# Attention half of an encoder layer: the stores of weight sums, residual rows and kept split weights issued by GpSimd and not by SyncE

## The chip, the cores and the metric

The kernel runs on one core of one Trainium2 chip. The metric is device time in microseconds for one launch. Engines are named as the profile names them: PE is TensorE (PEld its weight loads), DVE is VectorE, ACT is ScalarE, POOL is GpSimd, SP is SyncE, which here does nothing but issue transfers (SPq is its queue).

## The reference, cut to what matters

The reference computes one layer of a streaming encoder, for a prompt of 2048 tokens and a sample of 64 tokens, with d_model 1024, all in fp32:

```
mod = silu(c) @ w_ada + b_ada                      # six columns of scales and shifts
h    = rmsnorm(x, g1) * (1 + sc1) + sh1
proj = h @ w_in                                    # u, q, k, v, o, gates
pool = causal window means (2, 4, 8, 16) of u, minus u, @ w_pool, * s_pool
hs   = mLSTM(q, k, v, gates), chunk by chunk, normalized per head, * sigmoid(o)
x    = x + gt1 * (concat(pool, hs) @ w_out)        # end of the attention half
h2   = rmsnorm(x, g2) * (1 + sc2) + sh2
up   = h2 @ w_up                                   # 2 x 2816 columns
conv = causal depthwise convolution of width 3 over up
x    = x + gt2 * ((silu(g) * a) @ w_down)          # the gated MLP
y    = rmsnorm(x, g_final)
```

The states of the pooling, of the mLSTM and of the convolution are outputs too. The attention half is everything up to the first new x.

## The kernel before

**Number format.** Every large product runs as three products of rounded parts: a matrix is split into a high part (ACT copies it rounded, L366) and a low part (DVE subtracts, L369), and PE forms high times high, high times low, low times high.

**Attention half.** The tokens are worked on in four groups of 512 (the last with the 64 sample tokens). For each group: the value projection (L1114), for each of four heads the projections of q, k and o (L423) with the mLSTM of the head before woven between them, four blocks for the pooling mixer, then the output projection, row by row (`outproj`). The mLSTM of a head ends with a normalizer: DVE makes a sum per token (L1309 to L1311), POOL raises it to the power -1/2 (L1313), DVE scales the head's rows with it (L1315), and PE transposes them (L1326). PE, DVE and POOL each work through their instructions in order.

**Weights.** A stream of units of 512 columns is read in a fixed order. `issue` starts the load on SP: an unsplit unit into one of four `raw` tiles (L350), a unit that was split before straight into one of six `wt` tiles (L355). `work_out` splits it, `get_unit` hands it to the product. In group 0 the projection weights come unsplit and, once used, their split halves are stored to DRAM by `keep` (L374, tensor `hl_kept`, 40 stores of some 512 KB), and groups 1 to 3 load them from there. `keep` also serves the MLP's weights (`wsplit`), at a time when `spare` is no longer empty.

**Weight sums.** For the MLP's products the kernel needs sums and differences of blocks of w_up. `up_sums` makes them in the background of groups 1 to 3: it loads four blocks into one of five `w4` tiles (L846), DVE adds and subtracts (L867 to L871), and `store` writes the tile to the tensor `wsum` (L856, 44 stores of 512 KB). Its instructions are pinned to program order among each other.

**Residual rows.** `outproj` loads a row of x into one of five `scr` tiles (L546), DVE adds the projection (L596) and the row is stored to `x2d` (L598, 32 stores).

**What sets the order.** In group 0's first part and in the MLP the order is as written. In the rest of the attention half a scheduler orders each engine's instructions by its own estimate of times, so that a store that moves to another engine can move others too. Transfers are issued in each engine's order: an instruction that waits holds everything behind it.

Of the kernel before, what the change touches and what calls it, by code (L numbers as in the profile page):

```python
# [9 lines left out]
F32 = mybir.dt.float32  # L10
# [49 lines left out]
def tile_layer(ctx: ExitStack, tc: tile.TileContext, xT, vecs, cst, rst, rowv, w_mod, w_ada, w_qkou, w_v, w_pool,  # L60
               w_out, w_up, w_down, st_C, st_pool, yT, o_pool, o_C, o_m, o_conv):
    nc = tc.nc
    act, dve, pool, pe = nc.scalar, nc.vector, nc.gpsimd, nc.tensor
# [16 lines left out]
    def mm_ps():  # L80
        return bank("mm")
# [12 lines left out]
    def scr():  # L94
        return sp.tile([P, TMAX], F32, tag="scr", name="scr")
# [142 lines left out]
    for g in range(NG):  # L238
        o = Grp()
# [48 lines left out]
    wsum = dr.tile([NF, P, 4, 512], F32, tag="wsum", name="wsum")  # L288
# [21 lines left out]
    for g in range(NFG):  # L310
        for (f0, f1_) in PARTS:
# [8 lines left out]
            for i, (n, k) in enumerate(order):  # L320
                if i == f1_ - f0 - 2:
                    stream += late
                c = f0 + k // 4 * 4
# [9 lines left out]
    class Unit:  # L333

        state = 0
        w = raw = None
# [34 lines left out]

    def keep(u):
        if u.keep is not None:
            nc.sync.dma_start(out=u.keep, in_=u.w.bitcast(F32)[:, :, :u.n])  # L374

    def pump():

# [10 lines left out]
    def get_unit():  # L388
        if not pend:
            issue()  # L390
        u = pend.pop(0)
        work_out(u)
        keep(u)
        return u.w
# [18 lines left out]
    def gemm(ps, W, mv, o, ks=None, order=None, late=None, ups=(1, 3, 4, 6)):  # L413
        order = order or list(range(len(mv)))
        ks = ks or order
        for k in ks:
            if late is not None and k == late:
                drain(0, 2)
            at = order.index(k)
            U = W.at(at // 4)  # L420
            for pi, (a, b) in enumerate(PASSES):
                for bi, (lo, hi) in enumerate(o.blks):
                    pe.matmul(ps[bi][:, :hi - lo], U[:, a, k % 4 * P:(k % 4 + 1) * P], mv[k][:, b, lo:hi],  # L423
                              start=(at == 0 and pi == 0), stop=(k == order[-1] and pi == 2))
            if at in (1, 2, 4, 6, 7):
                tick(0)
            if at in ups and not quiet:
                tick(4)
            if at in (1, 3, 5) and o.last and not spare:
                tick(1)  # L430
            if at in ((2, 5) if o.g else (4,)) and not quiet and not spare:
                tick(3)
            if spare and at in (1, 3, 4, 6):
                tick(1)
        for i in (1, 3):
            tick(i)
        for gen in list(bg[2]):
            if next(gen, 0) == 0:
                bg[2].remove(gen)
# [12 lines left out]
    def sq_acc(ssum, src, T, first):  # L452
        if first:
            act.activation(ssum[:, :T], src, AF.Square)
        else:
            s = scr()
            act.activation(s[:, :T], src, AF.Square)
            dve.tensor_tensor(out=ssum[:, :T], in0=ssum[:, :T], in1=s[:, :T], op=ALU.add)

    def ssum_tile():  # L460
        return sp.tile([P, TMAX], F32, tag="ssum", name="ssum", bufs=1)
# [11 lines left out]
    def col_sums(pt, src, o, first, last):  # L473
        for ti, (lo, n, s) in enumerate(o.chunks):
            c, d = ti % 4 * 32, ti // 4 * P
            pe.matmul(pt[c:c + 32, d:d + n], ones[:, 0:32], src[:, lo:lo + n], start=first and ti < 4, stop=last,
                      skip_group_check=True)
# [58 lines left out]
    x2d = dr.tile([KD, P, NTOK], F32, tag="x2d", name="x2d")  # L536
# [7 lines left out]
    def load_x(k, o):  # L544
        x = scr()
        nc.sync.dma_start(out=x[:, :o.T], in_=xT[k, :, o.t0:o.t0 + o.T])  # L546
        return x
# [14 lines left out]
    def stat2(o, ssum, squares, pt):  # L562
        for _ in range(5):
            yield
        out = RS2[:, 4 * o.g:4 * o.g + len(o.chunks)]
        for n, t in squares:
            col_sums(pt, t, o, n == 0, n == KD - 1)
            yield
        yield from rstd_rows(ssum, o, out, pt)
        yield  # L570

    def outproj(o, mix, between):

        order = [4, 5, 6, 7, 3, 2, 1, 0]
        ssum = None if o.last else ssum_tile()
        squares, pt = [], None
        nx = [load_x(n, o) for n in (0, 1)]
        for rows in [(0, 1)] + [(n,) for n in range(2, KD)]:
            xs = nx
            Ws = [Row() for _ in rows]  # L580
            pss = [[mm_ps() for _ in o.blks] for _ in rows]
            if len(rows) == 1:
                gemm(pss[0], Ws[0], mix, o, order=order, ups=(4,))
            else:
                for W, ps in zip(Ws, pss):
                    gemm(ps, W, mix, o, ks=order[:6], order=order)
                quiet.clear()
                for W, ps in zip(Ws, pss):
                    gemm(ps, W, mix, o, ks=order[6:], order=order, late=1)
            while squares and squares[0][0] < rows[0] - (rows[0] < KD - 1):  # L590
                n, t = squares.pop(0)
                col_sums(pt, t, o, n == 0, False)
            nx = [load_x(rows[-1] + 1, o)] if rows[-1] + 1 < KD else []
            for n, x, ps in zip(rows, xs, pss):
                for (bi, pa, pb, a, b, s) in o.pieces:
                    dve.scalar_tensor_tensor(out=x[:, a:b], in0=ps[bi][:, pa:pb], scalar=gt1(n, s), in1=x[:, a:b],  # L596
                                             op0=ALU.mult, op1=ALU.add)
                nc.sync.dma_start(out=x2d[n, :, o.t0:o.t0 + o.T], in_=x[:, :o.T])  # L598
            if rows[0] == 0:
                between()  # L600
                if o.last:
                    pt = small.tile([P, 512], F32, tag="bank", name="m2")
            for n, x in zip(rows, xs):
                if o.last:
                    t = scr() if n < KD - 1 else fscr("ssum")
                    act.activation(t[:, :o.T], x[:, :o.T], AF.Square)
                    squares.append((n, t))
                else:
                    sq_acc(ssum, x[:, :o.T], o.T, n == 0)
        bg[0].append(stat2(o, ssum, squares, pt))  # L610

    fgroups = []
    for g in range(NFG):
        o = Grp()
# [8 lines left out]
    def fscr(dt=F32):  # L623
        if dt in ("rb", "rbn", "ssum"):
            return spare[0].tile([P, FT], F32, tag=dt, name=dt)
        return spare[0].tile([P, FT], dt, tag="fscr", name="fscr", bufs=6)
# [5 lines left out]
    spare = []  # L632
# [201 lines left out]
    if True:  # L834
# [6 lines left out]
        def up_sums():  # L841

            def load(f, c):
                w = a1.tile([P, 4, 256], F32, tag="w4", name="w4", bufs=5)
                for i in range(2):
                    tc.keep_in_program_order(nc.sync.dma_start(out=w[:, 2 * i:2 * i + 2, :], in_=w_up[NF * i + f].rearrange(  # L846
                        "p (h c) -> p h c", h=2)[:, :, c:c + 256]))
                return w
            todo = [(f, c) for f in range(NF) for c in (0, 256)]
            pin = tc.keep_in_program_order  # L850
            nx = [load(*todo[0]), load(*todo[1])]
            done = []

            def store():
                f, c, w = done.pop(0)
                pin(nc.sync.dma_start(out=wsum[f, :, :, c:c + 256], in_=w))  # L856
            yield
            yield
            for i, (f, c) in enumerate(todo):
                w = nx.pop(0)  # L860
                yield
                yield
                if len(done) > 1:
                    store()

                a0, a1_, g0, g1 = (w[:, i, :] for i in range(4))
                pin(dve.tensor_tensor(out=g1, in0=g0, in1=g1, op=ALU.add))  # L867
                pin(dve.tensor_tensor(out=g0, in0=a0, in1=g0, op=ALU.subtract))
                yield
                pin(dve.tensor_tensor(out=a0, in0=g1, in1=a0, op=ALU.subtract))  # L870
                pin(dve.tensor_tensor(out=a1_, in0=a1_, in1=a0, op=ALU.subtract))  # L871
                done.append((f, c, w))
                if i + 2 < len(todo):
                    nx.append(load(*todo[i + 2]))
                yield
            store()
            store()

        def rows_of(o):
# [519 lines left out]
        for o in groups:  # L1399
# [54 lines left out]
            if o.last:  # L1454
                bg[1].append(early_sums())
                outproj(o, mix, leave)
            else:
                bg[1].append(norm_apply(groups[o.g + 1], box, hn))
                outproj(o, mix, nothing)
# [474 lines left out]
```

## Time and profile before

| what | us |
|---|---|
| median of 3 runs (2209.5 to 2211.93) | 2210.5 |
| span of the profiled execution | 2205.6 |
| PE busy in it | 2186.1 |
| DVE busy | 1568.5 |
| ACT busy | 1005.3 |
| POOL busy | 203.0 |
| attention half, to the first product of the MLP | 800.0 |

The profiled execution's span runs from the first to the last instruction of the program; what lies around it is in the median alone. Times inside are counted from the start of the span. In the page's groups, a line such as L423 is a line of the kernel; in the waits, "A <- B: total, times, longest" says that engine A stood still until B released it. DMA queues: all transfers of the program go through SP's queue (468.05 MB) and ACT's (28.09 MB); POOL has none.

### The profile page before, as it was taken

The numbers are of one execution on the slowest core, as the hardware profiler recorded it, in microseconds if no ns is written. First come the engines' busy times: TensorE is split into PE (matmuls) and PEld (weight loads), VectorE is DVE, ScalarE is ACT, GpSimd is POOL, SyncE is SP. The second block draws the span as 40 slices with busy tenths as digits, with TensorE's granted clock in tenths as the row PEclk, the third lists the DMA queues.
The fourth block names the chain that finished last, engine by engine and source line by source line (L and its number), as shares of the span: only waits on it lengthen the run. The fifth ranks groups of instructions, "written<-read, shape, count | busy, mean of one in ns | idle before, by whom it ended". The sixth has DMA issues, their size and how long they took to land. (4 is left out here: it accounts for less than half of the span.)

```text
span 2205.6 us, 38165 instructions
## 1 busy us (share of the span) xinstructions
PE 2186.1 (99%) x13804; PEld 2079.2 (94%) x13804; DVE 1568.5 (71%) x2916; ACT 1005.3 (46%) x1993; POOL 203.0 (9%) x481
## 2 busy tenths in 40 slices
PE   8999999999999999999999999999999999999998
PEld 7888888888899999999999999999999999999998
DVE  5887669577765778787958587767667685767474
ACT  4653334235243455554636354545344443445354
POOL 0010000001000100010000210000001210101012
PEclk9999999999999999999999999999999999999999
DMA  9977987997898695767557876565458565353442
GB/s 355 367 242 264 333 275 243 324 324 239 292 323 272 223 310 177 234 205 239 188 173 233 266 245 200 183 214 175 144 169 285 186 190 166 111 173 121 150 148 81
DMA packets 279357, 498.58 MB, mean 226 GB/s; under 512 B 25176, under 2 KB 105432, under 8 KB 279168
## 3 DMA queue, kind: packets, MB, share of 16 engines
q1 hardware_dynamic: 267392, 468.05, 65.0%
q10 hardware_dynamic: 11776, 28.09, 3.4%
q8 instruction: 109, 1.79, 0.3%
q14 instruction: 80, 0.66, 0.1%
HBM read 385.29 MB, written 110.75 MB: 225 GB/s over the span
## 5 line engine op out<-in xcount | busy, mean ns | idle before, releaser
L1522 PE MATMUL mm<-hx,wt 128*128 128x352 f32 x5544 | 885.4, 321 | 1.0 <-DVE ea L1574 0.9
L1522 PEld LDWEIGHTS mm<-hx,wt 128*128 128x128 f32 x5544 | 879.5, 188 | 2.1 <-ACT wt L366 1.5
L1785 PE MATMUL mm<-av,wt 128*128 128x352 f32 (+2 forms) x3168 | 508.6, 321 | 0.4 <-DVE av L1645 0.3
L1785 PEld LDWEIGHTS mm<-av,wt 128*128 128x128 f32 x3168 | 502.6, 188 | 3.0 <-DVE av L1645 0.9
L423 PE MATMUL mm<-hl,wt 128*128 128x512 f32 (+2 forms) x1920 | 395.8, 358 | 1.7 <-DMA wt<-hl_kept 1.7
L366 ACT ACTIVATE wt<-raw 128x512 fp32r<-128x512 f32 (+3 forms) x494 | 274.5, 571 | 249.6 <-PE mm L1785 109.3
L369 DVE TENSOR_TENSOR wt<-raw,wt 128x512 fp32r<-128x512 f32 (+3 forms) x494 | 307.0, 637 | 87.5 <-ACT wt L366 81.4
L423 PEld LDWEIGHTS mm<-hl,wt 128*128 128x128 f32 x1920 | 312.6, 188 | 49.4 <-issue 5.3
L1800 DVE SCALAR_TENSOR_TENSOR x<-mm,MOD,x 128x352 f32<-128x352 f32 (+4 forms) x224 | 106.5, 526 | 128.8 <-PE mm L1785 128.8
L423 PE MATMUL mm<-mx,wt 128*128 128x512 f32 (+1 forms) x960 | 186.8, 353 | 0.0
L423 PEld LDWEIGHTS mm<-mx,wt 128*128 128x128 f32 x960 | 158.8, 188 | 25.4 <-ACT mx L1378 1.1
L1510 DVE SCALAR_TENSOR_TENSOR tg<-eg,V,tg 128x704 f32<-128x704 f32 (+1 forms) x132 | 125.7, 952 | 49.3 <-ACT tg L1505 46.8
L369 DVE TENSOR_TENSOR wt<-wt 128x512 fp32r<-128x512 f32 x176 | 121.8, 692 | 49.4 <-ACT wt L366 49.2
L366 ACT ACTIVATE wt<-wt 128x512 fp32r<-128x512 f32 x176 | 110.2, 626 | 75.1 <-DMA wt<-wsum 62.5
L1510 DVE SCALAR_TENSOR_TENSOR ta<-ea,V,ta 128x704 f32<-128x704 f32 (+1 forms) x132 | 125.6, 952 | 7.8 <-ACT ta L1505 5.4
L1645 DVE TENSOR_TENSOR av<-tg,av 128x704 fp32r<-128x704 f32 (+4 forms) x112 | 62.0, 588 | 43.2 <-ACT av L1637 43.0
L1570 ACT ACTIVATE u<-mm 128x352 f32<-128x352 f32 x66 | 30.6, 464 | 120.3 <-PE mm L1522 81.8
L1616 ACT ACTIVATE tg<-tg 128x704 f32<-128x704 f32 (+1 forms) x66 | 52.3, 793 | 68.9 <-DVE tg L1510 68.9
L203 DVE SCALAR_TENSOR_TENSOR acc<-raw,CA,acc 128x512 f32<-128x512 f32 x84 | 60.5, 744 | 32.1 <-DMA raw<-w_ada 32.1
L1530 DVE TENSOR_TENSOR eg<-mm,u 128x352 f32<-128x352 f32 x154 | 70.1, 467 | 18.4 <-ACT u L1585 11.2
L1114 PE MATMUL mm<-wt,hl 128*128 128x256 f32 (+1 forms) x576 | 70.9, 282 | 0.0
L1114 PEld LDWEIGHTS mm<-wt,hl 128*128 128x128 f32 x576 | 69.3, 188 | 1.0 <-issue 0.6
(299 smaller groups left out, 1951.9 us busy)
## 6 DMA issues: line engine op xcount, KB each, us to landing
wt<-hl_kept SPq DMA_DIRECT2D x108, 512.0 KB, 5.9
raw<-w_up SPq DMA_DIRECT2D x198, 256.0 KB, 3.1
wt<-wsum SPq DMA_DIRECT2D x176, 256.0 KB, 4.0
wt<-wsplit SPq DMA_DIRECT2D x88, 512.0 KB, 3.9
raw<-w_down SPq DMA_DIRECT2D x96, 256.0 KB, 3.9
w<-w_up SPq DMA_DIRECT2D x88, 256.0 KB, 5.4
wsum<-w SPq DMA_DIRECT2D x44, 512.0 KB, 5.7
wsplit<-wt SPq DMA_DIRECT2D x44, 512.0 KB, 5.0
```

What stands on the lines that cost most here:

```text
L203: dve.scalar_tensor_tensor(out=acc[s], in0=w, scalar=CA[:, k, s:s + 1], in1=acc[s], op0=ALU.mult, op1=ALU.add)
L366: act.activation(u.w[:, 0, :u.n], u.raw[:, :u.n], AF.Copy)
L369: dve.tensor_tensor(out=u.w[:, 1, :u.n], in0=u.raw[:, :u.n], in1=u.w[:, 0, :u.n].bitcast(F32), op=ALU.subtract)
L423: pe.matmul(ps[bi][:, :hi - lo], U[:, a, k % 4 * P:(k % 4 + 1) * P], mv[k][:, b, lo:hi], start=(at == 0 and pi == 0), stop=(k == order[-1] ...
L1114: pe.matmul(ps[ti][:n, :cols], h[4 * kh + k4][:, b, lo:lo + n], U[:, a, k4 % 2 * cols:(k4 % 2 + 1) * cols], start=(kh == 0 and k4 == 0 and ...
L1510: dve.scalar_tensor_tensor(out=t[:, :E], in0=ext[:, j:j + E], scalar=wc(j, f), in1=t[:, :E], op0=ALU.mult, op1=ALU.add)
L1522: pe.matmul(ps[:, :FH], U[:, a, kc * P:(kc + 1) * P], Bo.at(nm, kc, b), start=(first and kc == 0 and pi == 0), stop=(kc == 3 and pi == 2), ...
L1530: dve.tensor_tensor(out=ext[:, d:d + b - a], in0=ps[:, a:b], in1=u[:, a:b], op=ALU.add)
L1616: act.activation(self.tg[:, :E], self.tg[:, :E], AF.Silu)
L1645: dve.tensor_tensor(out=cut(1), in0=self.of_tg(cut(0), a, b), in1=cut(0).bitcast(F32), op=ALU.subtract)
L1785: pe.matmul(ps[i][:, :hi - lo], U[:, a, k % 4 * P:(k % 4 + 1) * P], av[k](b, lo, hi), start=(k == 0 and (a, b) == PASSES[0]), stop=(k == n ...
L1800: dve.scalar_tensor_tensor(out=x3[n][:, a:b], in0=ps[i][:, a - lo:b - lo], scalar=gt2(n, s), in1=x3[n][:, a:b], op0=ALU.mult, op1=ALU.add)
```

## The change

Three places that issue a store name POOL's queue and no longer SP's. `keep` does so only while `spare` is empty, which is the attention half.

```diff
     def keep(u):
         if u.keep is not None:
-            nc.sync.dma_start(out=u.keep, in_=u.w.bitcast(F32)[:, :, :u.n])
+            (nc.sync if spare else pool).dma_start(out=u.keep, in_=u.w.bitcast(F32)[:, :, :u.n])
...
-                nc.sync.dma_start(out=x2d[n, :, o.t0:o.t0 + o.T], in_=x[:, :o.T])
+                pool.dma_start(out=x2d[n, :, o.t0:o.t0 + o.T], in_=x[:, :o.T])
...
             def store():
                 f, c, w = done.pop(0)
-                pin(nc.sync.dma_start(out=wsum[f, :, :, c:c + 256], in_=w))
+                pin(pool.dma_start(out=wsum[f, :, :, c:c + 256], in_=w))
```

The scheduler's order changes with it. First place: POOL in group 0, from the first normalization to the end of the heads, before (sf is a head's normalizer, va the value tile; the number behind a name tells tiles apart).

```order
L471 TENSOR_TENSOR rs_251<-rs_251,half_111 128x4
L1104 MEMSET va_715 128x20
L1313 TENSOR_TENSOR sf_1017<-sf_1017,half_111 128x4
L1313 TENSOR_TENSOR sf_1248<-sf_1248,half_111 128x4
L1313 TENSOR_TENSOR sf_1483<-sf_1483,half_111 128x4
L1104 MEMSET va_2328 128x20
```

Now, around the first head's power (22 stores stand ahead of it, six between it and the next):

```order
L374 DMA hl_kept_128<-wt_1054 256x1x512
L374 DMA hl_kept_128<-wt_1097 256x1x512
L374 DMA hl_kept_128<-wt_1115 256x1x512
L1313 TENSOR_TENSOR sf_1017<-sf_1017,half_111 128x4
L374 DMA hl_kept_128<-wt_1146 256x1x512
L374 DMA hl_kept_128<-wt_1199 256x1x512
```

And DVE there now:

```order
L1309 TENSOR_TENSOR sf_1017<-nd_925 128x4
L1310 TENSOR_TENSOR sf_1017<-sf_1017,CL_891 128x4
L369 TENSOR_TENSOR wt_1115<-raw_1039,wt_1115 128x512
L1311 SCALAR_TENSOR_TENSOR sf_1017<-sf_1017,sq_973 128x4
L369 TENSOR_TENSOR wt_1146<-raw_1057,wt_1146 128x512
L1315 TENSOR_TENSOR nd_925<-nd_925,sf_1017 128x4x128
```

The store of wt_1115 waits for the split of that tile, which stands directly ahead of the last sum of the normalizer; it is the same for the second and the third head (with wt_1344 and wt_1569).

Second place: PE at the second head's transposes in group 0, as a piece of the difference.

```order
 L423 MATMUL mm<-hl_611,wt 128x512 x3
+L423 MATMUL mm<-hl_612,wt 128x512 x2
 L1326 MATMUL m_1301<-ident,nd 128x128 x4
-L423 MATMUL mm<-hl_612,wt 128x512 x3
+L423 MATMUL mm<-hl_612,wt 128x512
```

The four transposes stand two matmuls later. PE's order is otherwise as it was but for one other place.

Third place: POOL in group 1, now (before, the three powers stand one behind the other there).

```order
L498 TENSOR_TENSOR RS2_134<-RS2_134,half_111 128x4
L856 DMA wsum_129<-w4_2625 512x1x256
L856 DMA wsum_129<-w4_2628 512x1x256
L1313 TENSOR_TENSOR sf_2897<-sf_2897,half_111 128x4
L856 DMA wsum_129<-w4_2692 512x1x256
L856 DMA wsum_129<-w4_2753 512x1x256
L856 DMA wsum_129<-w4_2821 512x1x256
L1313 TENSOR_TENSOR sf_3135<-sf_3135,half_111 128x4
L856 DMA wsum_129<-w4_2924 512x1x256
L856 DMA wsum_129<-w4_2983 512x1x256
L856 DMA wsum_129<-w4_3013 512x1x256
L1313 TENSOR_TENSOR sf_3338<-sf_3338,half_111 128x4
```

The sums of w4_2692, whose last DVE instruction stands well ahead of the first head's normalizer, are stored behind its power. On SP the loads of the group's w4 tiles keep their places between the weight loads, without the stores.

## The prediction

> **What bounds the kernel now.** I read the busy table first. The profiled execution spans 2205.6 us; the median of the runs is 2210.5 us, so 4.9 us lie around the span and are added back at the end.
>
> ```profile
> span 2205.6 us, 38165 instructions
> PE 2186.1 (99%) x13804; PEld 2079.2 (94%) x13804; DVE 1568.5 (71%) x2916; ACT 1005.3 (46%) x1993; POOL 203.0 (9%) x481
> ```
>
> TensorE is busy in 99% of the span, so only time in which PE stands still can be won, and every new wait of PE is lost in full. The table by stretches cuts the span at the start-up, the rest of token group 0, groups 1 to 3, and the gated MLP; its columns are the stretch, its length, then the busy time and count of each engine.
>
> ```profile
> 0.00:55.00 55.00, 48.85 (x518) 40.59 (x519) 28.57 (x64) 23.22 (x44) 3.89 (x23) 1.00 0.98 355
> 55.00:180.00 125.00, 123.98 (x635) 102.11 (x634) 104.75 (x204) 70.14 (x162) 11.95 (x14) 1.00 0.84 294
> 180.00:800.00 620.00, 617.58 (x3855) 545.64 (x3853) 434.02 (x931) 240.50 (x582) 36.01 (x57) 1.00 0.86 286
> ```
>
> All moved stores belong to the attention half, whose last row of output is worked on near 800 us (the MLP's first product, quoted below, starts there). From 55 us to 800 us PE stands still for 1.02 + 2.42 = 3.4 us. Of the 6.2 us before 55 us, 4.5 us are the first wait for x, ahead of any store; the start-up's loads of modulation weights cost PE little (total, times, longest in us):
>
> ```profile
> PE m L994 <- DMA mx<-xT: 4.5, 1, 4.5
> ...
> PE m L941 <- DMA mx<-w_mod: 0.5, 2, 0.3
> ```
>
> So the change can win 3.4 us at most. PE's waits in 55 to 800 us:
>
> ```profile
> PE mm L423 <- DMA wt<-hl_kept: 1.7, 2, 1.3
> ...
> PE m L1326 <- DVE nd L1315: 0.2, 1, 0.2
> ```
>
> Only the first row, 1.7 us, hangs on SP's queue of loads. The last row is where the change can hurt.
>
> **What is taken from SP.** The 116 stores leave SP's order: 40 of kept weights (L374), 44 of weight sums (L856), 32 of residual rows (L598). SP had been held at them; from the waits of SP's queue:
>
> ```profile
> SPq L856 <- DVE w L871: 25.7, 7, 4.9
> SPq L598 <- DVE scr L596: 24.2, 23, 3.6
> ```
>
> These 50 us and the issuing itself free SP. But SP is not what PE waits for: in 180 to 400 us its longest wait is for PE to give up a weight slot.
>
> ```profile
> SPq L355 <- PE mm L423: 42.0, 29, 4.6
> ```
>
> SP stands ready before the slot is free, 29 times. What it wins by the stores going it then waits out at the next slot. I count 0 for it in the forecast, and -1.7 us (the hl_kept row) as its best, with -3.4 us for all waits as the outer bound.
>
> The DMA engines carry the same bytes; their share is 0.98, 0.84 and 0.86 in the three stretches, so another queue brings no bandwidth. [...]
>
> **What is put on POOL.** No row shows a POOL-issued DMA; its cost t is the unknown. The nearest rows are the same stores issued by SP (min/median/max ns), and their landing:
>
> ```profile
> L374 SPq DMA_DIRECT2D hl_kept<-wt x40: 331/580/1417, 31.9 to 150.1; - x40
> ```
> ```profile
> DMA to landing us min/median/max: 4.1/5.9/8.6
> ```
>
> Lower bound of t: 0.33 us, SP's quickest. Upper bound: 5.9 us, if POOL were held until the data has landed. I take 1.5 us, near SP's slowest issue (1.4 us). One reason to stay above SP's median is that POOL is itself disturbed beside VectorE. A copy of 16 columns takes 0.2 us at best, and 1.73 us here, where it starts 0.21 us after a run of split instructions on DVE does:
>
> ```profile
> 161.77 1.28 DVE L369 TENSOR_TENSOR wt<-raw,wt 128x512 fp32r<-128x512 f32 x2
> 161.98 1.73 POOL L1339 COPY u<-UH 128x16 f32<-128x16 f32 x1 [3.33 <-DVE scr L1366]
> ```
>
> [...]
>
> **Who waits behind a store.** POOL runs in order, and its power instruction (L1313) is the last step of a head's normalizer: DVE's L1315 waits for it, and PE's transposes L1326 for that. Everything in PE's order stands behind L1326. Group 0's first three heads, whose L1313 now comes directly behind a store, on POOL before:
>
> ```profile
> 81.85 1.45 POOL L1313 TENSOR_TENSOR sf<-sf,half 128x4 f32<-128x4 f32 x1 [67.50 <-DVE sf L1311]
> 102.42 1.01 POOL L1313 TENSOR_TENSOR sf<-sf,half 128x4 f32<-128x4 f32 x1 [19.12 <-DVE sf L1311]
> 124.42 1.45 POOL L1313 TENSOR_TENSOR sf<-sf,half 128x4 f32<-128x4 f32 x1 [20.99 <-DVE sf L1311]
> ```
>
> DVE's side, for head 1:
>
> ```profile
> 102.18 0.16 DVE L1311 SCALAR_TENSOR_TENSOR sf<-sf,sq 128x4 f32<-128x4 f32 x1 [0.52 <-ACT jk L1301]
> ...
> 103.46 0.69 DVE L1315 TENSOR_TENSOR nd<-nd,sf 128x512 f32<-128x512 f32 x1 [1.12 <-POOL sf L1313]
> ```
>
> In DVE's new order the weight split (L369) on which that store waits stands directly before L1311 in each of the three. So the store becomes ready one small DVE instruction, 0.16 us, before the power would, and the power starts t - 0.2 late. PE's transposes of the three heads, and what cover each has:
>
> ```profile
> 84.17 0.63 PE L1326 MATMUL m<-ident,nd 128*128 128x128 f32 x4 [0.22 <-DVE nd L1315]
> ```
> ```profile
> 105.43 0.60 PE L1326 MATMUL m<-ident,nd 128*128 128x128 f32 x4
> ```
> ```profile
> 126.74 0.63 PE L1326 MATMUL m<-ident,nd 128*128 128x128 f32 x4
> ```
>
> - head 0: PE already stands still 0.22 us there, no cover. Cost t - 0.2 = 1.3 us.
> - head 1: DVE ends at 104.15, PE comes at 105.43: 1.28 us. In the new order two more matmuls stand ahead of L1326. One lasts 55 us / 243 = 0.226 us by the row below, so 0.45 us more. Cost t - 0.2 - 1.7, below 0, so 0.
> - head 2: the power ends at 125.87, DVE's 0.69 us at 126.6, PE at 126.74: 0.1 us. Cost t - 0.3 = 1.2 us.
>
> ```profile
> 330.00:385.00 55.00, 55.00 (x243) 44.84 (x242) 51.07 (x86) 27.33 (x45) 4.19 (x8) 1.00 0.74 243
> ```
>
> In head 3 and in groups 1 to 3 the last store ahead of each L1313 waits for a DVE instruction that stands many places ahead of L1311, so it has been issued by then: 0. The sum is 1.3 + 0 + 1.2 = 2.5 us. At t = 0.33 it is 0.1 + 0 + 0 = 0.1 us; at t = 5.9 it is 5.7 + 4.0 + 5.6 = 15.3 us.
>
> **Stores that come later than before.** In groups 1 to 3 some sums now stand behind a power that waits for its head. The third store of group 1 is one; the row below it is the load that refills the same one of the five buffers:
>
> ```profile
> 258.37 0.56 SPq L856 DMA_DIRECT2D wsum<-w  x1
> ...
> 268.17 1.74 SPq L846 DMA_DIRECT2D w<-w_up  x2
> ```
> ```profile
> 264.04 1.39 POOL L1313 TENSOR_TENSOR sf<-sf,half 128x4 f32<-128x4 f32 x1 [40.45 <-DVE sf L1311]
> ```
>
> The store now goes at 265.4 instead of 258.4, lands by 265.4 + 1.5 + 5.7 = 272.6 (5.7 us is the first row below), and SP, in order, stands at the load 4.4 us longer; the weight loads behind it come as much later. The worst such place is the ninth store, whose power ends 308.1 and whose load went at 309.2: 308.1 + 7.2 = 315.3, 6.1 us. Cover: six weight slots of 12 matmuls, so five slots or 5 x 12 x 0.226 = 13.6 us from a slot's release to its use, less 5.9 us of landing (second row below), is 7.7 us. So 0; with 8.6 us, the slowest landing of the stores of the same size above, the cover is 5.0 us and such a place costs 1.1 us.
>
> ```profile
> wsum<-w SPq DMA_DIRECT2D x44, 512.0 KB, 5.7
> ```
> ```profile
> wt<-hl_kept SPq DMA_DIRECT2D x108, 512.0 KB, 5.9
> ```
>
> At the end of group 3, loads for the MLP's first sums wait until the last three stores have landed, because they take over their memory:
>
> ```profile
> 766.97 1.75 SPq L796 DMA_DIRECT2D fscr<-h2d  x4
> ...
> 789.72 0.96 DVE L748 TENSOR_TENSOR hx<-fscr,hx 128x352 fp32r<-128x352 f32 x2
> ...
> 800.00 5.97 PE L1522 MATMUL mm<-hx,wt 128*128 128x352 f32 x36
> ```
>
> The three stores now stand behind a residual row's store, so they can be issued only from 759.0 us on; with three times t and a landing the last is down at 769.2, 2.2 us after 766.97, against 800.0 - 790.7 = 9.3 us of cover. 0. In the start-up the first two stores can go near 21 us, not 32 us, ahead of loads; 1.06 MB at the stretch's 355 GB/s is 3 us of delay for weights of the modulation, a loss of at most that; I take 0, since PE's longest wait for those loads, quoted above, is 0.3 us.
>
> **The sum** is 2205.6 + 2.5 + 4.9 = 2213.0 us: a tenth of a per cent slower. About 0.2%, 4.4 us, is what a measurement of this kernel can tell from no change.
>
> **The rivals.**
> - *Relief:* SP's freed 50 us remove PE's waits. For it: 1.7 us of PE's idle time is a wait for hl_kept while SP had stores in its order. Against: 29 waits for slots. 2210.5 - 3.4 = 2207.1 us.
> - *POOL held by the transfer:* t is near 5.9 us, POOL stands until the data is down. 2210.5 + 15.3 = 2225.8 us. It is a measurable loss from t = 2.3 us on: 2.1 + 0.4 + 2.0 = 4.5 us. Against it: SP issues the same store in 0.58 us and doesn't stand for its landing of 5.9 us.
> - *Backlog:* DVE's instructions keep POOL from issuing, as they did the copy, and POOL cannot keep up in group 0: 40 stores in 21 to 150 us is one per 3.2 us. At t = 4 us it falls (4 - 3.2) x 40 = 32 us behind, weight slots stay held, ScalarE stops at its splits, PE behind it: about 2242 us. It decides from t = 3.2 us. Against it: DVE stands still while it waits for L1313, and so lets POOL catch up.
> - *Late sums:* the landing is near its slowest, and the late stores exceed their cover: three places in each of three groups at 1.1 us, less those covered, about 6 us, beside the 2.5: 2219 us. For it: PE waits 1.7 us for hl_kept even now, so that the cover isn't 7.7 us everywhere.
>
> **How the numbers follow.** Forecast 0.53, relief 0.10, held 0.17, backlog 0.08, late sums 0.12. The forecast's own range is 2207 to 2217 us (t from 0.33 us with the whole gain, to 3 us). The range for 8 in 10 reaches up to the held case: 2207 to 2226 us. Faster by over 0.2%: 3.4 us cannot reach 4.4 us except by an accident of the runs, 0.03. Slower by over 0.2%: held, backlog, late sums and the tail of the forecast above t = 2.3 us, 0.17 + 0.08 + 0.09 + 0.09 = 0.43. Within: 0.54.
>
> **What would show it.** Right: PE's waits at L1326 grow near 83 and 126 us by 1 to 1.5 us each, and nowhere else; L1313 in group 0 starts about 1.3 us after L1311; SP's waits at L846 for wsum grow, without PE waiting for hl_kept more:
>
> ```profile
> SPq L846 <- DMA wsum<-w: 7.9, 5, 2.7
> ```
>
>  Wrong: POOL's DMA rows last over 3 us, ACT's split L366 waits for stores of hl_kept, PE waits at L1326 in groups 1 to 3 or for hx at 800 us, or L423's waits for hl_kept grow. A time under 2207 us would mean that PE's idle time is not what limits this part.

## The result and the profile after

The changed kernel takes 2265.3 us (median of 4 runs, 2256.7 to 2267.6), the kernel before 2210.0 us beside it: a ratio of 1.0241, 95% interval 1.0226 to 1.0256. It is 55.3 us slower, where I had forecast 2213.0 us and a range that ended at 2226 us.

The busy table of the profile after:

```profile
span 2263.2 us, 38352 instructions
PE 2204.8 (97%) x13804; PEld 2091.9 (92%) x13804; DVE 1570.1 (69%) x2916; ACT 1002.9 (44%) x1993; POOL 274.8 (12%) x597
```

The span grew by 57.6 us. PE's busy time grew by 18.7 us (2204.8 - 2186.1) for the same 13804 matmuls, and its idle time by the other 38.9 us. So there are two kinds of loss: PE stands still, and PE works more slowly. The table by stretches of the kernel after (columns as in the prediction; behind POOL stand PE's granted clock, the DMA engines' share and GB/s) shows both in the attention half:

```profile
0.00:55.00 55.00, 48.30 (x498) 38.61 (x498) 26.43 (x60) 19.67 (x36) 10.42 (x33) 0.94 0.94 347
55.00:180.00 125.00, 113.52 (x576) 92.44 (x577) 92.90 (x182) 62.90 (x151) 28.92 (x42) 0.96 0.74 265
180.00:800.00 620.00, 595.87 (x3528) 521.07 (x3527) 415.84 (x878) 228.13 (x556) 80.08 (x123) 0.98 0.80 268
```

From 55 to 180 us PE stands still for 11.5 us (1.0 before), from 180 to 800 us for 24.1 us (2.4 before), and the granted clock, 1.00 before, is 0.96 and 0.98. The MLP's first product starts at 856.1 us and not at 800.0 us; behind it only 1.5 us are added. PE's waits in the attention half after, up to 860 us:

```profile
PE m L1216 <- ACT CL L1210: 11.6, 3, 6.8
PE m L1284 <- DVE kw L1264: 10.3, 4, 7.8
PE m L218 <- DVE kw L1264: 5.6, 1, 5.6
PE mm L423 <- DVE scr L596: 5.0, 1, 5.0
...
PE mm L423 <- ACT va L1127: 4.0, 2, 3.4
...
PE m L1326 <- DVE nd L1315: 0.8, 2, 0.4
```

The wait on which my sum rested, L1326, is the last row, 0.8 us. The large ones are for other steps of a head: its gate columns (L1208 on DVE, L1210 on ACT, then PE's L1216) and its weighted keys (L1264, then L1284). Neither step has an instruction on POOL. Around the first of them, on DVE, ACT and PE of the kernel after:

```profile
73.93 0.13 DVE L1174 COPY M<-M 4x1 f32<-4x1 f32 x1
...
76.68 0.88 DVE L201 TENSOR_SCALAR acc<-w,CA 128x512 f32<-128x512 f32 x2 [2.62 <-DMA w<-w_ada]
...
79.28 1.41 DVE L203 SCALAR_TENSOR_TENSOR acc<-w,CA,acc 128x512 f32<-128x512 f32 x2 [1.12 <-DMA w<-w_ada]
80.62 0.17 DVE L1208 COPY CL<-m 128x16 f32<-128x16 f32 x1
...
81.05 0.61 PE L1216 MATMUL m<-CL,C 128*128 128x16 f32 x2 [6.77 <-ACT CL L1210]
```

The same place in the kernel before:

```profile
67.41 0.13 DVE L1174 COPY M<-M 4x1 f32<-4x1 f32 x1
67.47 1.27 DVE L369 TENSOR_TENSOR wt<-raw,wt 128x512 fp32r<-128x512 f32 x2
68.67 0.15 DVE L1208 COPY CL<-m 128x16 f32<-128x16 f32 x1
...
69.10 0.39 PE L1216 MATMUL m<-CL,C 128*128 128x16 f32 x2 [0.81 <-ACT CL L1210]
```

Before, 1.3 us lie between L1174 and L1208; after, 6.7 us. The scheduler has put background sums on w_ada (L201, L203, four of them here) ahead of L1208, and DVE stands for their loads, in order. Most of the other long waits in groups 2 and 3 look alike: DVE stands up to 10.0 us for w_ada at L203 and up to 8.0 us for w_up at L867, with the head's step behind it.

The second thing that is new is on POOL and SP. In the kernel after, at the second place (460.8 us) where PE stands long:

```profile
449.45 0.72 POOL L856 DMA_DIRECT2D wsum<-w  x1 [16.44 <-DVE M L1174]
453.88 1.21 SPq L846 DMA_DIRECT2D w<-w_up  x2
454.13 0.71 POOL L856 DMA_DIRECT2D wsum<-w  x1 [3.97 <-issue]
458.71 1.20 SPq L846 DMA_DIRECT2D w<-w_up  x2
459.00 0.72 POOL L856 DMA_DIRECT2D wsum<-w  x1 [4.16 <-issue]
460.00 0.56 SPq L188 DMA_DIRECT2D raw<-w_ada  x1
```

A store of a weight sum lands, 4.4 to 4.7 us after its issue (SP's waiting load L846 goes that moment), and only 0.3 us later POOL issues the next one, although nothing that the profile shows holds it ("issue"). SP stands at each L846 for a landing, and the load of w_ada that DVE needs goes at 460.00, behind them. SP's wait of this kind in the whole span, 7.9 us before:

```profile
SPq L846 <- DMA wsum<-w: 81.0, 29, 5.3
```

### The profile page after: what moved, and what is told of

Same layout as the page of the kernel before. It is cut to its first block, busy times and chain, and to the rows that moved or that the text cites. A ratio compares the mean times of both kernels' runs of the same rounds, so it can differ in the third digit from the quotient of the medians.

```text
span 2263.2 us, 38352 instructions
## 1 busy us (share of the span) xinstructions
PE 2204.8 (97%) x13804; PEld 2091.9 (92%) x13804; DVE 1570.1 (69%) x2916; ACT 1002.9 (44%) x1993; POOL 274.8 (12%) x597
## 5 line engine op out<-in xcount | busy, mean ns | idle before, releaser
L423 PE MATMUL mm<-hl,wt 128*128 128x512 f32 (+2 forms) x1920 | 403.2, 363 | 4.0 <-ACT va L1127 4.0
L369 DVE TENSOR_TENSOR wt<-raw,wt 128x512 fp32r<-128x512 f32 (+3 forms) x494 | 306.6, 636 | 97.6 <-ACT wt L366 90.1
L423 PEld LDWEIGHTS mm<-hl,wt 128*128 128x128 f32 x1920 | 318.9, 192 | 53.0 <-issue 4.7
L423 PE MATMUL mm<-mx,wt 128*128 128x512 f32 (+1 forms) x960 | 189.1, 356 | 5.1 <-DVE scr L596 5.0
L423 PEld LDWEIGHTS mm<-mx,wt 128*128 128x128 f32 x960 | 161.0, 191 | 30.5 <-DVE scr L596 5.1
L369 DVE TENSOR_TENSOR wt<-wt 128x512 fp32r<-128x512 f32 x176 | 121.6, 691 | 47.9 <-ACT wt L366 47.7
L203 DVE SCALAR_TENSOR_TENSOR acc<-raw,CA,acc 128x512 f32<-128x512 f32 x84 | 59.9, 743 | 45.0 <-DMA raw<-w_ada 45.0
```

The lines of the kernel that those rows point to most:

```text
L203: dve.scalar_tensor_tensor(out=acc[s], in0=w, scalar=CA[:, k, s:s + 1], in1=acc[s], op0=ALU.mult, op1=ALU.add)
L369: dve.tensor_tensor(out=u.w[:, 1, :u.n], in0=u.raw[:, :u.n], in1=u.w[:, 0, :u.n].bitcast(F32), op=ALU.subtract)
```

## The experiments

Three suspects follow: the **order** of the engines' instructions, which the scheduler changed; the **ring**, a scratch that the kernel sets to 1024 bytes, by which POOL's stores of sums may come to wait for each other's landing, as in the rows above; and **late sums**, stores of weight sums that stand on POOL behind a head's power. All kernels compute the whole layer. Losses are against the kernel before, in the same comparison (its medians were 2208.4 to 2210.0 us).

| run | order | wsum pinned | scratch | stores on POOL | median us | loss us |
|---|---|---|---|---|---|---|
| the change | scheduler's | yes | 1024 | all | 2265.3 | 55.3 |
| e1 | scheduler's | yes | 2048 | all | 2250.1 | 40.1 |
| e2 | of before | yes | 1024 | all | 2237.1 | 27.2 |
| e3 | of the change | on SP | 1024 | none | 2294.2 | 84.3 |
| e4 | of before | yes | 2048 | all | 2234.7 | 24.7 |
| e5 | of before | on SP | 1024 | kept, rows | 2212.1 | 3.0 |
| e6 | of before | yes | 1024 | sums | 2232.7 | 23.6 |
| e7 | of before | no | 2048 | all | 2209.1 | 0.0 |
| e8 | of the change but for one place | yes | 1024 | all | 2265.0 | 55.9 |
| e9 | scheduler's | no | 1024 | all | 2237.1 | 28.7 |
| e10 | scheduler's | no | 2048 | all | 2230.9 | 22.4 |
| e11 | of before | no | 1024 | all | 2212.5 | 4.1 |
| e12 | scheduler's | on SP | 1024 | kept | 2222.9 | 14.5 |
| e13 | of e12 but for one place | on SP | 1024 | kept | 2221.4 | 11.7 |
| e14 | of before | no | 2048 | sums | 2207.6 | -2.1 |
| e15 | of before | no | 2048 | sums, rows | 2208.5 | -1.2 |

**The ring (e1).** One number:

```diff
-    nc = _bacc.Bacc("TRN2", ..., dynamic_dma_scratch_size=1024)
+    nc = _bacc.Bacc("TRN2", ..., dynamic_dma_scratch_size=2048)
```

> [...] The order on every engine stays that of the changed kernel. In the changed kernel's trace a weight-sum store of 512 pieces always starts 0.3 us after the one before it has landed (458.70 landed, 459.00 next), and SP's loads of w4 tiles wait 81.0 us for such stores. Theory 'full ring': the scratch holds the descriptors of one such store, POOL stands until it is down, the next w4 load and everything behind it on SP come late, and DVE and PE behind them. It expects two stores in flight, SP's waits for wsum under 35 us, and most of the loss after 180 us (56.1 - 18 = 38 us) gone: 2220 to 2240 us. Theory 'order': the scheduler put DVE's background sums (L203, L867) ahead of the heads' own steps, so DVE stands for loads that land later than it assumed; the ring doesn't matter. It expects 2255 to 2268 us.

2250.1 us, a ratio of 1.0188 (1.0170 to 1.0206): 15.2 us better than the change and between the two expectations. The same three stores of sums as above, on POOL with the larger scratch:

```profile
445.49 2.20 POOL L856 DMA_DIRECT2D wsum<-w  x3 [22.82 <-DVE M L1174]
473.17 1.20 POOL L1313 TENSOR_TENSOR sf<-sf,half 128x4 f32<-128x4 f32 x1 [25.48 <-DVE sf L1311]
474.33 1.46 POOL L856 DMA_DIRECT2D wsum<-w  x2
```

Three go within 2.2 us where they took 10.3 us (449.45 to 459.72). SP's wait at L846 falls from 81.0 to 56.6 us, not to the 35 expected. So the size of the scratch sets how soon the next store goes, and it is the smaller part of the loss; what the scratch holds, no run shows.

**The order, by itself (e2, e3).** The order of a built kernel is written down as a table of instruction names; each instruction is then issued behind the one ahead of it in the table, without a wait for its end:

```diff
-        tile_layer(tc, w_v=w_v, **a, **b)
+        tile_layer(tc, w_v=w_v, **a, **b); _pin(tc, _order())
+def _pin(tc, order):
+    by = {i.name: i for i in tc.nc.cur_bb.bb.instructions}
+    info = mybir.DependencyInfo(mybir.DependencyClass.NoSync, mybir.DependencyReason.DATA)
+    for engine, names in order.items():
+        mine = [by[f"I-{n}"] for n in names if f"I-{n}" in by]
+        mine = [i for i in mine if str(i.engine).split(".")[-1] == engine]
+        for a, b in zip(mine, mine[1:]):
+            tc.add_manual_dep(b, a.name, info, reason="order")
```

> The changed kernel, stores on POOL, but with the order of the kernel before written down for PE, ACT, DVE, POOL's own work and SP (SP without the stores), and only the places of the stores on POOL left to the scheduler. Theory 'order': DVE no longer stands for background loads ahead of the heads' steps; 2209 to 2220 us, my forecast's own 2.5 us at most and a little more. Theory 'full ring': POOL's stores still wait for each other's landing, the w4 loads still come late, and DVE stands for them all the same; 2235 us or more.

> The kernel before, stores on SP, but with the changed kernel's order written down for PE, ACT, DVE and POOL's own work; SP's order is the scheduler's. Theory 'order': the loss is there without any store on POOL; 2240 us or more. Theory 'full ring': without POOL's ring there is no loss; 2209 to 2220 us. If both have a share, group 0 (no weight sums there) tells the share of the order: 18 us of loss by 150 us in the changed kernel.

e2: 2237.1 us, 1.0127 (1.0106 to 1.0148). The number falls to the side of "full ring" (2235 us or more), and yet 28.1 us of the loss went with the order, half of it. So neither theory is enough. What is written down is the order of every engine, SP's loads too: between the kernel before and the change, DVE runs another instruction at 399 of the 2918 places of its order, and SP another at 313 of the 1366 places that both have. So the 28.1 us are the price of all of it, and no run parts DVE's share from SP's. In group 0 the order is most of the loss: in e2 the fourth head's transposes (L1326) start at 152.0 us. In the kernel before and in the change they start here:

```profile
149.75 0.60 PE L1326 MATMUL m<-ident,nd 128*128 128x128 f32 x4
```
```profile
167.67 0.60 PE L1326 MATMUL m<-ident,nd 128*128 128x128 f32 x4
```

Of 17.9 us, 15.7 go with the order and 2.2 stay. The other 25 us of e2's loss come behind 450 us. e3: 2294.2 us, 1.0378 (1.0359 to 1.0397), so the loss is there with not one store on POOL, 11.6 us of it by the same point. It is larger than the change's own: PE now also waits at the value projection for the residual rows, which it does not in the change. I read this as an order that was made for an SP without stores and fits an SP with them still less; no run tests it:

```profile
PE mm L1114 <- DVE scr L596: 23.1, 3, 10.4
```

**Both (e4).** The old order and 2048 bytes:

> Both: stores on POOL, the order of the kernel before written down, scratch of 2048 bytes. Full ring: as quick as the kernel before within 5 us, 2208 to 2216 us, and clearly quicker than the old order with 1024 bytes. Order: the same as the old order with 1024 bytes, 2209 to 2220 us. If it stays over 2225 us a third cause is at work, POOL's own cost of 0.69 us for a store or its place ahead of the normalizers' power.

2234.7 us, 1.0117 (1.0099 to 1.0134). Only 2.4 us better than e2: neither order nor ring is the rest, and a third cause was at work, as the last sentence of the expectation says. SP still stood 93.3 us at L846, once for 11.0 us.

**Which stores (e5, e6).** Old order, with wsum back on SP, and with wsum alone on POOL:

```diff
-                pin(pool.dma_start(out=wsum[f, :, :, c:c + 256], in_=w))
+                pin(nc.sync.dma_start(out=wsum[f, :, :, c:c + 256], in_=w))
```

> The order of the kernel before written down, as in the run with the old order, but the weight sums are stored by SP again; only kept weights and residual rows are on POOL. In the run with the old order and 1024 bytes the loss is 2.2 us by 150 us and the other 24 come from 450 us on, where SP stands at loads of w4 tiles for wsum stores that stand behind a head's power on POOL. Theory 'late sums': without wsum on POOL 2211 to 2217 us is left, the 2.2 us of group 0 and little more. Rival 'any store on POOL': residual rows cost too, as SP's loads wait 16.0 us for x2d there (4.0 before); 2225 us or more.

> The counterpart: only the weight sums are stored by POOL, kept weights and residual rows by SP, order of the kernel before written down. Late sums: nothing lost by 240 us (under 0.5 us), then nearly the whole loss of the run with all three on POOL; 2228 to 2238 us, PE waiting for hl_kept loads. Any store on POOL: 2220 us or less.

e5: 2212.1 us, 1.0016 (1.0007 to 1.0025). e6: 2232.7 us, 1.0108 (1.0091 to 1.0125). Both as "late sums" had it. How it comes about, on the four engines of e6 near 700 us:

```profile
692.01 1.03 POOL L1313 TENSOR_TENSOR sf<-sf,half 128x4 f32<-128x4 f32 x1 [13.77 <-DVE sf L1311]
...
694.74 0.55 POOL L1313 TENSOR_TENSOR sf<-sf,half 64x1 f32<-64x1 f32 x1 [1.70 <-DVE sf L1311]
...
695.34 0.74 POOL L856 DMA_DIRECT2D wsum<-w  x1
...
698.67 1.21 SPq L846 DMA_DIRECT2D w<-w_up  x2
698.97 0.72 POOL L856 DMA_DIRECT2D wsum<-w  x1 [2.89 <-issue]
700.63 2.00 SPq L355 DMA_DIRECT2D wt<-hl_kept  x2
...
706.47 1.78 PE L423 MATMUL mm<-hl,wt 128*128 128x256 f32 x6 [3.11 <-DMA wt<-hl_kept]
```

Read it from the top. POOL stands 13.8 us for the first power and 1.7 us for the second, with the stores of sums behind them, although DVE had ended the last L871 ahead of them at 688.7; the first store goes at 695.34 and is down at 698.67. There SP, which had issued its last transfer at 689.4, gets past its load of a w4 tile; the weights behind that load are issued at 700.63, and PE waits 3.1 us for them. SP's waits at L846 are 111.9 us in e6, the longest 10.1 us; in e5 4.5 us.

**Why the stores stand there (e7).** One word:

```diff
-                pin(pool.dma_start(out=wsum[f, :, :, c:c + 256], in_=w))
+                pool.dma_start(out=wsum[f, :, :, c:c + 256], in_=w)
```

`pin` ties an instruction behind whatever was written last for its own engine. While the store was SP's, that was another transfer of SP. Once it is POOL's, it is POOL's last instruction, and that is often a head's power.

> Old order, 2048 bytes, all three on POOL, and the wsum store no longer pinned behind what was written before it on its engine. On SP that was a load; on POOL it is a head's power (L1313), so the pin itself puts two of three stores behind the power. Without it the scheduler puts the third store of each four ahead of the power. Late sums through the pin: SP's waits at L846 for wsum fall from 93.3 to 60 us or less and 10 us or more of the 24.7 us that are left come back; 2215 to 2225 us. If the stores are late for another reason (ring, POOL's own pace): 2230 to 2238 us.

2209.1 us, 1.0003 (0.9993 to 1.0012): all 24.7 us that e4 had lost are back, more than expected, and no difference from the kernel before is left. All engines but POOL keep the written order in both, so what differs is where the stores stand on POOL. POOL's order in group 1 without the pin, with three sums ahead of the first power and not two:

```
L856 DMA wsum<-w4_2625 512x1x256
L856 DMA wsum<-w4_2628 512x1x256
L856 DMA wsum<-w4_2692 512x1x256
L1313 TENSOR_TENSOR sf<-sf,half 128x4
L856 DMA wsum<-w4_2753 512x1x256
L856 DMA wsum<-w4_2924 512x1x256
L856 DMA wsum<-w4_2821 512x1x256
L856 DMA wsum<-w4_2983 512x1x256
L1313 TENSOR_TENSOR sf<-sf,half 128x4
```

SP's wait at L846 is 36.0 us, and PE's for weights nearly gone (view of the waits of e7, SP in the whole span, PE from 55 to 860 us):

```profile
SPq L846 <- DMA wsum<-w: 36.0, 8, 8.8
```
```profile
PE mm L423 <- DMA wt<-hl_kept: 0.4, 1, 0.4
```

**The causes one at a time in the change (e9, e10, e11, e12).** The same edit as e7's in the change itself, with 1024 and with 2048 bytes, then with the old order and 1024 bytes; and the line of `keep` alone of the three, order left to the scheduler:

> The changed kernel, order left to the scheduler, 1024 bytes, with one edit: the wsum store is not pinned. Theory 'two causes': the pin sets the loss of groups 1 to 3 (it cost all 25 us under the old order), the scheduler's order of DVE that of group 0, where there are no wsum stores. So 14 to 18 us of loss at 150 us as before the edit, and under 12 us more behind it: 2228 to 2242 us. Rival 'order everywhere': the order of DVE in groups 1 to 3, which still puts sums on w_ada ahead of L1208, costs as much without the pin; 2250 us or more.

> The same with 2048 bytes. Two causes: stores that come in time meet the ring less often; 2 to 10 us less than without the larger ring, 2224 to 2236 us, and the loss at 150 us down to some 13 us as in the first run with the larger ring. Order everywhere: 2240 us or more.

> Old order written down, wsum store not pinned, 1024 bytes: what the ring costs by itself when the stores stand in time. If the ring matters: SP's waits for wsum rise from 36.0 to 60 us or more and 3 to 8 us are lost, 2212 to 2217 us. If the pin was all: 2208 to 2211 us, as with 2048 bytes.

> The kernel before with the first of the three lines alone: kept weights are stored by POOL, sums and rows by SP, order left to the scheduler. It gives DVE in group 0 the changed kernel's order (L201 and L203 ahead of L1208) and leaves the later groups nearly as they were. Order: 12 to 18 us of loss at 150 us and nothing behind it, 2222 to 2228 us. Rival 'POOL's store alone': the 2.7 us that kept weights and rows cost with the old order, 2211 to 2214 us.

2237.1 us (1.0129, 1.0114 to 1.0144), 2230.9 us (1.0104, 1.0088 to 1.0121), 2212.5 us (1.0019, 1.0009 to 1.0028) and 2222.9 us (1.0064, 1.0047 to 1.0081): e9 and e10 as "two causes" had it, e12 as "order", and e11's time as it was expected if the ring matters. In e9 14.5 us are lost by the fourth head and 13.6 more by the MLP, a little over the 12 expected, so the new order also costs something in groups 1 to 3 (on DVE it differs from the change's at 90 places, since the scheduler makes it anew without the pin). In e11 SP's wait rose to 42.5 us only, not to 60. Pin and order make a square: 55.3 us with both, 28.7 without the pin, 27.2 without the order, 4.1 without either; the pin is worth 26.6 us beside the new order and 23.1 us beside the old, the order 28.1 us with the pin and 24.6 us without, so that they nearly add up. The ring costs 15.2 us where both are there and 2.4 to 6.3 us elsewhere.

e12 shows the new order of group 0 without the sums on POOL. Its first head waits like that of the change, with the sums still on SP (waits of PE, 55 to 180 us):

```profile
PE m L1216 <- ACT CL L1210: 6.3, 1, 6.3
```

The same stores with the old order (e5, which has the rows on POOL too) lose 3.0 us and wait 0.6 us there.

**One place of the order (e8, e13).** In the change and in e12, with everything else of their order written down, the sums on w_ada of the first head were moved: in e8 nine of them (the expectation counts seven) behind a later step of the head, in e13 each to where the kernel before has it, up to L1311. DVE's order in e8:

```diff
-L201 L201 L369 L203 L203 L1208 L203 L1217 L203 L203 L203 L1264 L1256 L369 L1275 L1289 L203 L1289 L369 L1289
+L369 L1208 L1217 L1264 L1256 L369 L1275 L1289 L1289 L369 L1289 L201 L201 L203 L203 L203 L203 L203 L203 L203
```

> The changed kernel with its own order written down on every engine but for one place on DVE: the seven background sums on w_ada (L201, L203) that stand between L1174 and the last L1289 of the first head come behind that L1289. In the changed kernel PE stands 6.8 us there, at L1216, for L1208, which stands behind an L201 that waits for its load. Order: that wait falls under 1.5 us, and the kernel gains 5 to 7 us, 2258 to 2260 us. If DVE's place in line is only where late loads are felt, the sums are as late behind it, the wait comes back at the next head's steps, and the time stays at 2263 us or more.

> Kept weights alone on POOL (2222.9 us), its own order written down but for the first head on DVE: each sum on w_ada (L201, L203) up to L1311 stands where the kernel before has it against the head's steps. The same four engines and SP otherwise. PE waits 6.3 us at L1216 there and then runs at about half its clock for 5 us (0.54 and 0.78 in the two stretches of 5 us behind it), 3.4 us more. Order: 7 to 10 us come back, 2213 to 2216 us. If the late loads hit another step wherever the sums stand: 2220 us or more.

2265.0 us (1.0249, 1.0233 to 1.0266) and 2221.4 us (1.0050, 1.0037 to 1.0064): both gain nothing or next to nothing, against "order" as I had put it. The wait at L1216 did fall to 0.7 us, but it came back. In e8 my block of sums stood ahead of the head's fourth L1289 and kept PE 4.5 us at L1295. In e13 it came at the normalizer:

```profile
87.33 0.69 DVE L369 TENSOR_TENSOR wt<-raw,wt 128x512 fp32r<-128x512 f32 x1 [2.94 <-ACT wt L366]
...
88.60 0.15 DVE L1311 SCALAR_TENSOR_TENSOR sf<-sf,sq 128x4 f32<-128x4 f32 x1
...
89.28 3.40 DVE L203 SCALAR_TENSOR_TENSOR acc<-w,CA,acc 128x512 f32<-128x512 f32 x5
92.59 0.68 DVE L1315 TENSOR_TENSOR nd<-nd,sf 128x512 f32<-128x512 f32 x1
...
93.42 1.09 PE L1326 MATMUL m<-ident,nd 128*128 128x128 f32 x4 [6.33 <-DVE nd L1315]
```

A split (L369) ahead of L1311 waits 2.9 us, and five sums that my edit left ahead of L1315 take 3.4 us. So the order as a whole costs group 0 11.4 us (its fourth head's transposes start at 163.8 us in e12 and at 152.4 us in e5), but neither place that I moved accounts for it. DVE's new order has work that waits for loads ahead of several steps of the head. Which of these would have to go was not found out. A rival stands untested beside it, SP's own order of loads, which e13 kept: in e12 six loads of `raw` go ahead of the w_ada loads at 96.1 us, where e5 has four and issues these loads at 84.7 us.

**What SP's freed time is worth (e14, e15).** Sums, then sums and rows, on POOL without pin, 2048 bytes, old order, kept weights on SP:

> Only the weight sums on POOL, not pinned, 2048 bytes, order of the kernel before written down. Relief: SP's loads no longer stand behind stores that wait for DVE; PE's 2.4 us of idle time from 180 to 800 us go, 2205 to 2208 us. No worth: 2208 to 2211 us, the same as the kernel before.

> The same with the residual rows on POOL too. Relief: as much or a little more, 2205 to 2208 us. No worth: 2208 to 2211 us. If rows on POOL land too late for SP's loads of the same scr tiles (17.3 us of waits at L546 where all three were on POOL, 4.0 before): slower than without them by 1 us or more.

2207.6 us, 0.9992 (0.9983 to 1.0001), and 2208.5 us, 0.9996 (0.9987 to 1.0005). Both medians are below the kernel before, both intervals hold 1. PE's waits for hl_kept (1.7 us before) no longer show in e14, so the gain may be there; if so, it is about 2 us or less, and no version here beats the kernel before by what can be told.

## Why the prediction was wrong

- **What bounds, and what can be won.** Right. With the old order, the pin gone and the larger scratch, moving all three stores is worth 0.0 us (e7), and moving the sums alone or with the rows 2.1 or 1.2 us that can't be told from nothing (e14, e15). One reading was short: SP had been held at L856 and L598 not for 50 us, the two largest rows, but for some 92 us with the smaller ones (`SPq L856 <- DVE w L867: 15.3, 5, 6.2` is the next). The sum gave this time no worth, so it doesn't change.
- **POOL's cost of a store, t = 1.5 us.** Too high: the medians are 0.69 us for kept weights, 0.72 us for sums and 0.54 us for rows, the longest 0.91 us. The copy that took 1.73 us beside DVE's splits had kept my t above SP's median of 0.58 us; none of the 116 stores took as long, and a copy of the same size beside an equal run of splits took 0.53 us (kernel before, 525.23 us). But my bounds asked only whether a store holds POOL until it has landed itself. That the *next* store of a sum goes only once this one has landed, 0.3 us after it with 1024 bytes of scratch, was not in them.
- **The power behind a store, 2.5 us in group 0.** The mechanism is right. In the change the first head's power starts 0.9 us after L1311 ends (forecast 1.3):

```profile
95.72 0.15 DVE L1311 SCALAR_TENSOR_TENSOR sf<-sf,sq 128x4 f32<-128x4 f32 x1
96.21 0.67 POOL L374 DMA_DIRECT2D hl_kept<-wt  x1 [4.64 <-DVE sf L1311]
96.80 1.14 POOL L1313 TENSOR_TENSOR sf<-sf,half 128x4 f32<-128x4 f32 x1
```

  With the old order group 0 loses 2.1 to 3.1 us by its fourth head (e2, e4, e5, e7, e11), and e5 as a whole 3.0 us. But only 0.3 to 1.9 us of that are lost between the first head's L1216 and there; the rest, 0.4 to 2.7 us, is lost before that, in a part that I took at 0. That these losses add up to nearly the forecast 2.5 us is luck.
- **Stores that come later, 0 us.** This is the first step that failed. I priced one store at a time: 7.2 us from the power's end to the landing, at worst 6.1 us of standing for SP, against 7.7 us of cover. In e6 two or three finished sums stand behind the power, each goes only when the one before is down (at 698.97 us, 0.3 us after 698.67 us, in the rows above), and SP stands up to 10.1 us at one load and 111.9 us in all. That is over the cover, and measured 23.6 us, four times the 6 us of the rival "late sums". That one goes only when the one before is down isn't needed for it: with the larger scratch (e4) two go at once, and SP still stands up to 11.0 us at one load. I had the rows of POOL's new order before me, and did not ask what had put the stores behind the power: the pin.
- **The end of group 3, 0 us.** Wrong too: SP stands 7.5 us at L796 for the last sums, not 2.2, and the cover that I counted, up to the MLP's first product, was the wrong one. DVE waits 8.1 us for those loads while PE needs DVE's L596 for the output projection: 5.0 us, the row of L596 above.
- **The sum had no term for the engines' new order.** This is the second step that failed, and it is as large: 28.1 us (the change against e2, which gives back the order of SP's loads too). I had read the difference of the orders for what stands next to L1313 and to the stores, and for PE. That sums on w_ada stand ahead of L1208 in DVE's new order was plain to see, and was the same question as with the stores: what does this instruction wait for, and who is behind it? That the scheduler does it because its own estimate has the loads earlier once SP has no stores is argued; no run shows its estimates.
- **The price of a wait.** "Every new wait of PE is lost in full" was too cheap. Of the 57.6 us, 18.7 are the same matmuls taking longer, 18.3 of them in the attention half, where the granted clock is 0.94 to 0.98.
- **The signs.** POOL's DMA rows stay under 3 us, right; SP's waits at L846 grow, right, from 7.9 to 81.0 us, and L423 does not wait for hl_kept more, right too; PE's waits at L1326 do not grow by 1 to 1.5 us, and PE waits for other steps of the heads, which I had not listed.

## What to carry to other kernels

When an instruction moves to another engine, ask of every ordering tie it carries what it is tied to there: the same word that kept a store between two transfers put it behind a compute step. When a scheduler re-orders the rest, read the new order of the engine that feeds the bottleneck for work that waits for background loads and now stands ahead of the critical steps; the new order, and not the moved instructions, can be half the change. And price a wait of PE of a few us with the slow matmuls that can follow: here, by an estimate, 2.7 us on top of one of 6.8 us.

## What the hardware showed

**PE's granted clock fell with waits of a few us.** Stretches of 5 us around the first long wait of the kernel after (74.3 to 81.1 us; columns as above):

```profile
70.00:75.00 5.00, 3.49 (x17) 2.31 (x15) 3.93 (x7) 4.07 (x7) 1.95 (x3) 1.00 0.76 234
75.00:80.00 5.00, 0.00 (x0) 0.00 (x0) 2.20 (x5) 0.00 (x0) 0.76 (x2) 0.62 1.02 381
80.00:85.00 5.00, 3.95 (x12) 3.26 (x13) 3.60 (x8) 1.38 (x7) 0.00 (x0) 0.50 1.03 370
85.00:90.00 5.00, 5.00 (x31) 4.62 (x30) 3.98 (x8) 1.74 (x5) 0.67 (x1) 0.85 0.49 173
```

The granted clock is 0.50 for the 4 us behind the wait; matmuls of L423 take 0.50 us each there (2.48 us for five, from 81.50 us) and 0.27 us each from 88.14 us on (1.63 us for six). So a wait of 6.8 us costs some 2.7 us more, an estimate from the last two rows (half of 3.95, and 0.15 x 5). In the same trace the clock fell behind waits of 2.35 us (up to 454.44 us: 0.50 from 456 to 458 us) and 2.49 us (up to 665.73 us: 0.50 from 667 to 669 us), and stayed at 1.00 behind waits of 1.8 and 1.95 us (from 273.2 and 54.5 us). No one length of the wait decides: at the start it is 0.50 from 15 to 20 us, with no wait over 0.61 us since PE's first matmul at 4.81 us.

**POOL's stores of sums (512x1x256) waited for each other with the smaller scratch.** With 1024 bytes a store that stood ready went 0.3 us after the one before it had landed (458.71 and 459.00 us in the kernel after); with 2048 bytes three went within 2.2 us (e1). What a store waits for there the profile calls "issue"; only the run with the other size tells that it hangs on the scratch.
